# Linear attention's first head pair: TensorE's order written out, projections between its steps, two tiles' counts and the masks' last step on ScalarE

## The chip, the core and the metric

The kernel runs on one core of a Trainium2 chip. TensorE (PE) multiplies, VectorE (DVE), ScalarE (ACT) and GpSimd (POOL) do the rest, and SyncE (SP) issues transfers. Each engine works through its own instructions in the order in which they were built, and an instruction waits on semaphores until what it reads is there. The metric is the device time of one execution in microseconds (us); lower is better.

## The reference

One decoder layer over 1024 tokens of width 1024. What matters here is the first half: one projection feeds a sparse attention (group A), whose keys are chosen by an indexer's score, and a gated linear attention (group B).

```python
h = rmsnorm(x, norm1_g[l])
qa, ka, va, iq, ik, iw, qb, kb, vb, g_lr, r_gate = jnp.split(h @ w_in[l], split_points, axis=-1)
# group A: score = sum over 8 heads of relu(iq . ik) * iw, causal; the 256 best keys of each query are kept
_, idx = lax.top_k(score, topk)
...
# group B, in chunks: decayed attention inside a chunk, and a running state
log_a = jax.nn.log_sigmoid(g_lr @ gla_gate_w2[l] + gla_gate_b[l]) / GATE_TEMP
o_inter = einsum(qc * exp(b), state);  o_intra = einsum(attn, vc)       # b = cumsum(log_a)
state = exp(b_last) * state + einsum(kc * exp(b_last - b), vc)
o_b = rmsnorm(o_b, gla_out_norm_g[l]) * silu(r_gate)
x = x + concat([o_a, o_b]) @ w_out[l]
x = x + hier_moe(rmsnorm(x, norm2_g[l]), ...)                            # 32 experts
```

## The kernel before, in words

The 1024 tokens are 8 tiles of 128 (`t` = 0 to 7). The stage in question lies between the indexer's scores and the sparse attention, and three kinds of work meet in it.

**Projections.** `project_steps` makes one tile's projection onto 384 columns in 24 matmuls of 128x384 (weights split in a high part `wh` and a low part `wl`, 8 slices of each) into a PSUM tile `pj`, of which there are two. `load_w` brings a weight set in by DMA, makes `wh` on ACT (L259) and `wl` on DVE or POOL (L260). Of group B there are four sets: `qkv` and `vr`, for head pair 0 and head pair 1. `evac_qkv` copies a qkv projection out on ACT (`gq`, L402); `evac_vr` takes ACT for the value half and the output gate and ends on DVE (`gv`, L412).

**The linear attention** of a head pair `p` runs in four units `u` of two tiles. `gla1(p, u)` prepares: transposes of q and k (L616, L617), of the gate's low-rank input (L627), one gate matmul (L632), then a chain on ACT (`zb`, `l`: L636 to L639), DVE (`zb`, `l`, two cumulative sums `b` and `bc`: L641 to L647), POOL (ten subtractions `dd`: L653 to L658), ACT (exponentials: L660, L661) and DVE again (products with q and k: L669 to L675). `gla2(p, u)` uses them: five levels of small matmuls (L692 four times, L696), whose results DVE merges into `at` (L700, L705) and which take turns in three PSUM tiles `mm`; then the values and the state (L722, L725, L729; DVE updates the state at L733), the norm, and a `finish` that transposes the output (L752) and is called one unit later.

**The search.** For tiles 2 to 7 a threshold on the scores is searched in 7 rounds, `search(0)` to `search(6)`. A round counts, for each of the six tiles, the keys at or above a trial value (L512, one DVE instruction over 128 x (t+1)*128 with a sum, plus a read of that sum), and some 12 instructions on 128x6 choose the next value (L514 to L541). Rounds 0 to 4 count on a bf16 copy of the scores, 5 and 6 on the scores. `search_end` and `make_mask` then build each tile's mask; its last step is L578, on DVE.

What sets the order: inside a block `tc.manual_schedule(engines={PE})` PE's instructions keep the order in which they are written. Elsewhere a scheduler orders every engine by its own estimates. Before, the scoring ahead of this stage is such a block, with the rest of pair 0's qkv projections and all of its vr projections at its end; pair 0 of the linear attention, with pair 1's qkv projections and half of its vr projections, is not; pair 1 is again, and there a helper `weave` gives each step of `gla2` a room in nanoseconds that is filled with projections. Anything that is not PE's is the scheduler's throughout.

## Time and profile before

| | us |
|---|---|
| runs shown | 1091.1, 1083.46, 1087.89 (median 1087.89) |
| the profiled execution | 1083.67 |
| its span, first to last instruction | 1081.8 |
| PE busy | 997.9 (92%) |
| DVE busy | 777.4 (72%) |
| ACT busy | 657.3 (61%) |
| POOL busy | 387.7 (36%) |

The runs differ by 7.6 us, 0.7%. The stage that changes runs from the last matmul of the scores at 103.3 us to the first level matmul of pair 1 at 266.75 us. Times of rows are counted from the span's start. TensorE's granted clock is 1.00 at 2.4 GHz and 0.50 at 1.2 GHz.

### The profile page before, as it was taken

The page shows a single profiled execution, that of the slowest core. Times are in us where ns is not written, and L with a number is a line of the kernel's source. Part 1 is how long each engine was busy: PE and PEld are TensorE (multiplying, and loading weights), DVE is VectorE, ACT ScalarE, POOL GpSimd, SP SyncE. Part 2 cuts the span into 40 slices and gives each one's busy share as a digit, 9 for nine tenths or more (in the row PEclk, how much of TensorE's full clock was granted, in tenths as well). Part 3 has the DMA queues.
Part 4 walks back from the last instruction along what each step waited for, and adds up shares of the span by engine and source line. Part 5 has one row for each costly group of instructions (what it writes and reads, how often), then busy time and mean ns, then how long its engine had stood idle before and what let it go on. Part 6 is the DMA issues. An engine that isn't in the chain of part 4 may idle for free.

```text
span 1081.8 us, 17953 instructions
## 1 busy us (share of the span) xinstructions
PE 997.9 (92%) x5839; PEld 808.1 (75%) x5839; DVE 777.4 (72%) x2058; ACT 657.3 (61%) x1636; POOL 387.7 (36%) x497
## 2 busy tenths in 40 slices
PE   7799999989999999999989999949999999999993
PEld 7689888868888888988877878836666666666552
DVE  6877999874675666777775666667877777787772
ACT  7788643344655566666755533327877777777661
POOL 4510433641522224245442201154435444344321
PEclk9999999979999899999999999968999999999996
DMA  8210201020201202012231369869999999999983
GB/s 249 81 60 1 59 20 50 11 69 21 55 25 40 65 8 67 10 40 69 76 82 58 105 241 380 305 229 292 330 308 324 328 330 309 336 325 330 342 241 45
DMA packets 83204, 170.87 MB, mean 158 GB/s; under 512 B 14856, under 2 KB 45760, under 8 KB 82976
## 3 DMA queue, kind: packets, MB, share of 16 engines
q1 hardware_dynamic: 75936, 148.01, 40.6%
q0 software_dynamic: 7168, 21.65, 9.3%
q8 instruction: 48, 0.79, 0.3%
q14 instruction: 52, 0.43, 0.1%
HBM read 148.23 MB, written 26.88 MB: 162 GB/s over the span
## 4 chain that ended last, share of the span: by engine, by line
PE 57%; DMA 16%; DVE 14%; ACT 5%; issue 5%; POOL 1%; SPq 0%; POOLq 0%; DVEq 0%; ACTq 0%
PE pj L272 18%; DMA out_dram<-y,idx 9%; PE pj L1119 8%; DMA w<-in_w_exp_up_dram 4%; PE po L945 3%; PE mm L1493 3%; PE pj L1444 2%; PE pj L1446 2%; PE pj L1445 2%; DVE jb L512 2%; PE tp L933 2%; DVE w L1367 2%; DMA w<-in_w_exp_down_dram 2%; PE mm L1140 1%; PE mm L692 1%
## 5 line engine op out<-in xcount | busy, mean ns | idle before, releaser
L272 PE MATMUL pj<-wh,w 128*128 128x384 f32 (+1 forms) x1152 | 324.4, 348 | 7.2 <-DVE gv L412 6.1
L272 PEld LDWEIGHTS pj<-wh,w 128*128 128x128 f32 x1152 | 212.6, 194 | 15.6 <-DVE gv L412 7.6
L1366 ACT ACTIVATE w<-w 128x512 fp32r<-128x512 f32 x320 | 191.6, 627 | 45.7 <-PE mm L1446 27.9
L1367 DVE TENSOR_TENSOR w<-w,w 128x512 fp32r<-128x512 f32 x283 | 186.7, 698 | 31.5 <-ACT w L1366 28.2
L272 PE MATMUL pj<-wl,w 128*128 128x384 f32 (+1 forms) x576 | 200.1, 347 | 1.1 <-POOL wl L260 1.1
L272 PEld LDWEIGHTS pj<-wl,w 128*128 128x128 f32 x576 | 112.2, 195 | 4.5 <-POOL wl L260 1.3
L1444 PE MATMUL pj<-w,xT 128*96 128x512 f32 x256 | 105.7, 413 | 0.7 <-ACT w L1366 0.7
L1445 PE MATMUL pj<-w,xT 128*96 128x512 f32 x256 | 102.2, 399 | 1.6 <-DVE w L1367 1.1
L1446 PE MATMUL pj<-w,xT 128*96 128x512 f32 x256 | 102.0, 399 | 0.0
L1119 PE MATMUL pj<-w,mhl 128*128 128x512 f32 x384 | 101.1, 403 | 0.0
L910 POOL TENSOR_TENSOR cb<-bt,maskb 128x256 f32<-128x256 f32 (+1 forms) x64 | 43.5, 681 | 121.2 <-DVE mx L921 102.6
L1518 POOL DMA_INDIRECT out_dram<-y,idx x30 | 52.5, 1749 | 94.8 <-ACT w L1366 41.5
L260 POOL TENSOR_TENSOR wl<-wr,wh 128x384 fp32r<-128x384 f32 x58 | 60.8, 1070 | 61.9 <-ACT wh L259 61.6
L1119 PEld LDWEIGHTS pj<-w,mhl 128*128 128x128 f32 x384 | 69.4, 189 | 12.8 <-DVE mhl L1111 0.4
L1493 PE MATMUL mm<-w,hT 128*96 128x512 f32 x128 | 66.9, 605 | 0.5 <-ACT hT L1483 0.5
L1367 POOL TENSOR_TENSOR w<-w,w 128x512 fp32r<-128x512 f32 x37 | 50.4, 1361 | 46.5 <-ACT w L1366 36.0
L924 ACT ACTIVATE z<-z,mx 128x128 f32<-128x128 f32 (+7 forms) x64 | 49.5, 774 | 21.9 <-DVE mx L921 21.6
L1444 PEld LDWEIGHTS pj<-w,xT 128*96 128x96 f32 x256 | 44.1, 172 | 15.2 <-ACT w L1366 1.5
L1446 PEld LDWEIGHTS pj<-w,xT 128*96 128x96 f32 x256 | 41.9, 164 | 18.1 <-DVE xT L1458 0.2
L1445 PEld LDWEIGHTS pj<-w,xT 128*96 128x96 f32 x256 | 41.9, 164 | 17.2 <-DVE w L1367 2.6
L1454 PEld LDWEIGHTS tp<-cf,xg 96*128 96x128 f32 x256 | 40.9, 209 | 15.0 <-issue 8.5
L1444 PE MATMUL mm<-w,hTt 128*96 128x512 f32 x64 | 51.4, 804 | 0.0
(375 smaller groups left out, 2157.6 us busy)
## 6 DMA issues: line engine op xcount, KB each, us to landing
w<-in_w_exp_gate_dram SPq DMA_DIRECT2D x64, 512.0 KB
w<-in_w_exp_up_dram SPq DMA_DIRECT2D x64, 512.0 KB
w<-in_w_exp_down_dram SPq DMA_DIRECT2D x64, 512.0 KB
wr<-in_w_in_dram SPq DMA_DIRECT2D x80, 128.0 KB
xt<-in_x_dram SPq DMA_DIRECT2D x16, 512.0 KB
mt<-mixd SPq DMA_DIRECT2D x8, 512.0 KB
out_dram<-xt SPq DMA_DIRECT2D x8, 512.0 KB
h2d<-h SPq DMA_DIRECT2D x7, 528.0 KB
```

Of the source, the lines that this page charges most:

```text
L260: (V if by[kk + k] == "V" else G).tensor_tensor(b, raw[:, k], f32(a), op=OP.subtract)
L272: T.matmul(ps[:, :width], x_, y_[k], start=(k == 0 and i == 0), stop=(k == KC - 1 and i == 2))
L910: G.tensor_tensor(cb[:, :near], bts[p][:, i, 256 - near:], mask(t, far, L), op=OP.add)
L924: A.activation(z[:, :L], z[:, :L], AF.Exp, bias=mn, scale=-1.0, accum_out=sums[:, i:i + 1])
L1119: T.matmul(ps, lhs[:, k % 4], w[k, c], start=(k == 0 and i == 0), stop=(k == KC - 1 and i == 2))
L1366: A.activation(a, u, AF.Copy)
L1367: (G if engine == "G" else V).tensor_tensor(b, u, f32(a), op=OP.subtract)
L1444: T.matmul(ps, x[0], y[0], start=first, stop=False)
L1445: T.matmul(ps, x[0], y[1], start=False, stop=False)
L1446: T.matmul(ps, x[1], y[0], start=False, stop=last)
L1493: T.matmul(pd[:n], hT0, parts[2 * hf], start=True, stop=False)
L1518: G.indirect_dma_start(out=out[0], out_offset=bass.IndirectOffsetOnAxis(ap=idx[:CAP, e:e + 1], axis=0), in_=y[:CAP], in_offset=None, compu ...
```

## The change

1. The vr projections of pair 0 no longer stand at the end of the scoring block: that block now ends when pair 0's vr weights are loaded (`yield 0, "v"`).
2. Pair 0 of the linear attention becomes a written order of PE (`first_pair`), with what is left of the earlier filler, pair 1's qkv projections and half of its vr projections between its steps (`first_fill`). Each step of `gla2` gets 4.6 times its nominal room; the steps of `gla1` get their nominal room. A projection is held back until the step that frees its buffers has been written (`ended`).
3. `evac_qkv` copies q and k (`gq`) and v (`gw`) out with two ACT instructions in place of one.
4. In rounds 0 to 4 of the search the counts of tiles 6 and 7 (896 and 1024 keys) move to ACT, as a sum of signs; one DVE instruction on 128x2 turns the sums into counts.
5. The last step of each mask moves to ACT (a Relu with a large bias in place of a comparison and a product).

The constant behind the large bias is left out of the diff here.

```diff
@@ -74,6 +74,8 @@
 SHARE = (None, (1, 1, 1, 1, 1, 1, 0.85, 1.3), (1, 1, 1, 1, 1, 1, 0.85, 1.3), (1, 1, 1, 1, 1, 1, 1, 1.3))
 ROOM = (2.2, 2.8, 3.15, 3.3)
 OROOM = (0, 0, 0, 6000, 6000, 6000, 6000, 6000, 0)
+ROOM0 = (4.6, 4.6, 4.6, 4.6)
+MORE = 3
 LOG_FLOOR = -21.0 * 16.0
 LEVELS = (64, 32, 16, 8)
 BUCKET_START = [0, 1, 2, 3, 4, 5, 6, 7, 8, 9, 10, 11, 12, 13, 14, 15, 16, 19, 21, 24, 27, 31, 35, 40, 46, 52, 59,
...
@@ -234,7 +239,7 @@
     wp = p_h.enter_context(tc.tile_pool(name="wp", bufs=WBUFS, side="right"))
     hT = []
     p2 = ExitStack()
-    gqp = p2.enter_context(tc.tile_pool(name="gqp", bufs=10, side="right"))
+    gqp = p2.enter_context(tc.tile_pool(name="gqp", bufs=1, side="right"))
 
     p1 = ExitStack()
     scp = p1.enter_context(tc.tile_pool(name="scp", bufs=1, side="left"))
@@ -387,7 +392,7 @@
                         base=0, channel_multiplier=1)
 
 
-    gq, gv, pools = {}, {}, {}
+    gq, gw, gv, pools = {}, {}, {}, {}
 
     def qkv_load(p):
         c = p * P
@@ -398,8 +403,11 @@
         return load_w([(VB + 2 * c + P, P), (RG + 2 * c, 2 * P)], by=BY_VR[p])
 
     def evac_qkv(p, t, pj):
-        gq[p, t] = gqp.tile([P, 384], F32, name="gq", tag="gq", bufs=9)
-        A.activation(gq[p, t], pj[:, :384], AF.Copy, scale=rstd[:, t:t + 1])
+
+        gq[p, t] = gqp.tile([P, 256], F32, name="gq", tag="gq", bufs=NT)
+        gw[p, t] = gqp.tile([P, P], F32, name="gw", tag="gw", bufs=NT + MORE)
+        A.activation(gq[p, t], pj[:, :256], AF.Copy, scale=rstd[:, t:t + 1])
+        A.activation(gw[p, t], pj[:, 256:384], AF.Copy, scale=rstd[:, t:t + 1])
 
     def evac_vr(p, t, pj):
         g = pools["gvp"].tile([P, 384], F32, name="gv", tag="gv", bufs=NT)
@@ -455,6 +463,7 @@
                 index_operands(NT - 1)
                 yield 1000, NT - 1
         w = vr_load(0)
+        yield 0, "v"
         for t in range(NT):
             for ns in project_steps(t, w, lambda ps: evac_vr(0, t, ps)):
                 yield ns, 0
@@ -478,7 +487,7 @@
             score_sums(t)
             if t == 3:
                 relative_bias()
-        for _ in fill:
+        while next(fill)[1] != "v":
             pass
 
     p1b.close()
@@ -503,14 +512,29 @@
     V.tensor_tensor(st["v"], st["sd"], cf[:, CF_ZQ:CF_ZQ + 6], op=OP.mult)
     V.tensor_tensor(st["v"], st["v"], st["mean"], op=OP.add)
 
+    keys2 = srp.tile([P, 2], F32, name="keys2", bufs=1)
+    for t in range(6, NT):
+        G.memset(keys2[:, t - 6:t - 5], (t + 1) * P / 2)
+
     def search(it):
 
 
+        far = range(6, NT) if it < NROUND else ()
+        for t in far:
+
+            j = t - 2
+            jk = srp.tile([P, S], BF, name="ja", tag="ja", bufs=1)
+            A.activation(jk[:, :(t + 1) * P], mask(t), AF.Sign, bias=st["v"][:, j:j + 1], scale=-1.0,
+                         accum_out=st["c"][:, j:j + 1])
         for t in range(2, NT):
             j = t - 2
+            if t in far:
+                continue
             jk = srp.tile([P, S], BF, name="jb", tag="jb")
             V.tensor_scalar(jk[:, :(t + 1) * P], mask(t) if it < NROUND else acc[t], st["v"][:, j:j + 1], None,
                             op0=OP.is_ge, op1=OP.add, accum_out=st["c"][:, j:j + 1])
+        if far:
+            V.scalar_tensor_tensor(st["c"][:, 4:6], st["c"][:, 4:6], -0.5, keys2, op0=OP.mult, op1=OP.add)
         V.tensor_scalar(gei, st["c"], TARGET, None, op0=OP.is_ge)
         V.tensor_scalar(lti, st["c"], TARGET, None, op0=OP.is_lt)
         if it == NROUND:
@@ -575,7 +599,8 @@
         V.copy_predicated(k8, kp, m8)
         b2 = srp.tile([P, S], F32, name="b2", tag="jk")
         V.match_replace(b2[:, :L], k8, b1[:, :L], MARK)
-        V.tensor_scalar(mask(t), b2[:, :L], MARK_T, -NEG, op0=OP.is_gt, op1=OP.mult)
+
+        A.activation(mask(t), b2[:, :L], AF.Relu, scale=4e-9, bias=big)
 
 
     st_s = [glp.tile([P, P], F32, name=f"st_s{p}") for p in range(2)]
@@ -603,7 +628,7 @@
             room += ns
             while room > 0:
                 ns = next(fill, None)
-                if ns is None:
+                if not ns:
                     room = 0
                     break
                 room -= ns
@@ -717,7 +742,7 @@
         po = [ps[:, :2 * P].rearrange("p (i t) -> p i t", i=2) for ps in (ps_po(), ps_mm())]
         s = st_s[p]
         for i, t in enumerate(ts):
-            vals = (gq[p, t][:, 2 * P:], gv[p, t][:, :P])
+            vals = (gw[p, t], gv[p, t][:, :P])
             for h in range(2):
                 T.matmul(po[h][:, i], a[:, h, i], vals[h], start=True, stop=(t == 0))
             for h in range(2):
@@ -757,31 +782,59 @@
 
         gla_out[p] = finish
 
-    run(gla1(0, 0))
-    search(0)
-    search(1)
-    w = qkv_load(1)
-    run(gla1(0, 1))
-    for u in range(4):
-        run(gla2(0, u))
-        project_qkv(1, 2 * u, w)
-        project_qkv(1, 2 * u + 1, w)
-        if u < 2:
-            search(2 * u + 2)
-            search(2 * u + 3)
-            run(gla1(0, u + 2))
-        elif u == 2:
-            search(6)
-            search_end()
-            run(gla1(1, 0))
-    gla_out.pop(0)()
-    run(gla1(1, 1))
-    make_mask(2)
-    make_mask(3)
-    make_mask(4)
-    w = vr_load(1)
-    for t in range(4):
-        project_vr(1, t, w)
+    ended = [0, 0]
+
+    def first_pair():
+        yield from gla1(0, 0)
+        search(0)
+        search(1)
+        yield from gla1(0, 1)
+        ended[1] = 2
+        for u in range(4):
+            for ns in gla2(0, u):
+                yield ns * ROOM0[u]
+            ended[0] = u + 1
+            if u < 2:
+                search(2 * u + 2)
+                search(2 * u + 3)
+                yield from gla1(0, u + 2)
+                ended[1] = u + 3
+            elif u == 2:
+                search(6)
+                search_end()
+                yield from gla1(1, 0)
+        yield 2000
+        gla_out.pop(0)()
+        yield from gla1(1, 1)
+
+    ws = {}
+
+    def first_fill():
+
+        for ns, _ in fill0:
+            yield ns
+        w = qkv_load(1)
+        for t in range(NT):
+            while t >= MORE and ended[0] <= (t - MORE) // 2 or ended[1] <= t // 2:
+                yield 0
+            for ns in project_steps(t, w, lambda ps: evac_qkv(1, t, ps)):
+                yield ns if t else 2 * ns
+        w = ws["vr"] = vr_load(1)
+        for t in range(4):
+            while ended[0] <= t // 2:
+                yield 0
+            for ns in project_steps(t, w, lambda ps: evac_vr(1, t, ps)):
+                yield ns if t else 2 * ns
+
+    fill0 = fill
+    with tc.manual_schedule(engines={mybir.EngineType.PE}):
+        fill = first_fill()
+        weave(first_pair(), fill)
+        make_mask(2)
+        make_mask(3)
+        make_mask(4)
+        run(fill)
+    w = ws["vr"]
     for t in range(5, NT):
         make_mask(t)
```

**PE, behind the second gate matmul (u = 1) of pair 0, before.** `tp<-glT` is the gate matmul, `pj` rows are projections, `w4` and `w8` hold a tile's activations.

```order
L632 MATMUL tp_2000<-glT_2001,w2_106 128x256
L272 MATMUL pj_1613<-wh_1510,w4_255 128x384
L272 MATMUL pj_1613<-wl_1511,w4_255 128x384
L272 MATMUL pj_1613<-wh_1510,w4_256 128x384
L272 MATMUL pj_1613<-wh_1514,w4_255 128x384
L272 MATMUL pj_1613<-wl_1515,w4_255 128x384
L272 MATMUL pj_1613<-wh_1514,w4_256 128x384
L272 MATMUL pj_1613<-wh_1521,w4_255 128x384
L272 MATMUL pj_1613<-wl_1522,w4_255 128x384
L272 MATMUL pj_1613<-wh_1521,w4_256 128x384
```

These are the first nine of 24 projections that stand between that gate matmul and the first level matmul (L692).

**PE at the same place, after.** L657 is the gate matmul, L717 the level matmul, L277 the projection, L642 and L652 the last transposes of u = 1.

```order
L642 MATMUL tp_1726<-cf_64,gq_1339 128x128
L652 MATMUL tp_1733<-cf_64,glr_107 16x128 x2
L277 MATMUL pj_1625<-wh_1530,w8_133 128x384
L277 MATMUL pj_1625<-wh_1537,w8_133 128x384
L277 MATMUL pj_1625<-wl_1538,w8_133 128x384
L277 MATMUL pj_1625<-wh_1537,w8_133 128x384
L277 MATMUL pj_1625<-wh_1541,w8_133 128x384
L657 MATMUL tp_1733<-glT_1734,w2_106 128x256
L717 MATMUL mm_1788<-dd_1646 128x64
L717 MATMUL mm_1789<-dd_1646 128x64
L717 MATMUL mm_1788<-dd_1646 128x64
L717 MATMUL mm_1789<-dd_1646 128x64
```

The level matmuls of unit 0 now stand directly behind the gate matmul; the first gate matmul (u = 0) stands ahead of the rows shown, with five projections between the two, where 48 stood before.

**DVE, at the first gate's `zb`, before.** L512 is a count of round 0, L641 `zb` of unit 0, L646 its cumulative sum.

```order
L512 TENSOR_SCALAR jb,st_c<-maskb,st_v 128x640
L512 TENSOR_SCALAR jb,st_c<-maskb,st_v 128x768
L512 TENSOR_SCALAR jb,st_c<-maskb,st_v 128x896
L260 TENSOR_TENSOR wl<-wr,wh 128x384
L512 TENSOR_SCALAR jb,st_c<-maskb,st_v 128x1024
L641 SCALAR_TENSOR_TENSOR zb<-zb,l 128x256
L514 TENSOR_SCALAR gei<-st_c 128x6
L515 TENSOR_SCALAR lti<-st_c 128x6
L526 TENSOR_SCALAR st_num<-st_c 128x6
L642 TENSOR_SCALAR l<-zb 128x256
L646 SCALAR_TENSOR_TENSOR b<-zb 128x128 x2
```

The first gate's `zb` comes right behind round 0's counts.

**DVE at the same place, after.** L554 and L555 are the last steps of round 0, L534 a count of round 1, L666 `zb` of unit 0, L671 and L672 its cumulative sums.

```order
L552 TENSOR_TENSOR st_num<-st_num,st_sd 128x6
L553 TENSOR_TENSOR st_v<-st_v,st_num 128x6
L554 TENSOR_TENSOR st_v<-st_v,st_lo 128x6
L555 TENSOR_TENSOR st_v<-st_v,st_hi 128x6
L534 TENSOR_SCALAR jb,st_c<-maskb,st_v 128x384
L534 TENSOR_SCALAR jb,st_c<-maskb,st_v 128x512
L534 TENSOR_SCALAR jb,st_c<-maskb,st_v 128x640
L534 TENSOR_SCALAR jb,st_c<-maskb,st_v 128x768
L666 SCALAR_TENSOR_TENSOR zb<-zb,l 128x256
L667 TENSOR_SCALAR l<-zb 128x256
L671 SCALAR_TENSOR_TENSOR b<-zb 128x128 x2
L672 SCALAR_TENSOR_TENSOR bc<-l 128x128 x2
```

It now comes behind all of round 0 and the counts of round 1, which are four in place of six.

**ACT, on the first gate's chain, before.** L636 to L639 are the gate's four steps.

```order
L636 ACTIVATE zb<-tp,gs 128x256
L259 ACTIVATE wh<-wr 128x384 x2
L637 ACTIVATE l<-zb 128x256
L259 ACTIVATE wh<-wr 128x384
L638 ACTIVATE l<-l 128x256
L639 ACTIVATE l<-l 128x256
L619 ACTIVATE qk<-tp 128x512
L628 ACTIVATE glT<-tp 16x256
L663 ACTIVATE eb<-b 128x256
```

**ACT at the same place, after.** L661 to L664 are those four steps, L527 the counts by sign: the first row is round 0's second count, the other two are round 1's.

```order
L527 ACTIVATE ja,st_c<-maskb,st_v 128x1024
L661 ACTIVATE zb<-tp,gs 128x256
L644 ACTIVATE qk<-tp 128x512
L264 ACTIVATE wh<-wr 128x384
L662 ACTIVATE l<-zb 128x256
L653 ACTIVATE glT<-tp 16x256
L663 ACTIVATE l<-l 128x256
L527 ACTIVATE ja,st_c<-maskb,st_v 128x896
L664 ACTIVATE l<-l 128x256
L527 ACTIVATE ja,st_c<-maskb,st_v 128x1024
L688 ACTIVATE eb<-b 128x256
```

Round 1's first count stands ahead of the gate's last step (L664).

## Rows read from the trace of the kernel before

**Rows 1.** The page: the span, and TensorE's granted clock in 40 slices.
```profile
span 1081.8 us, 17953 instructions
...
PEclk9999999979999899999999999968999999999996
```

**Rows 2.** Busy us (xinstructions) of PE, PEld, DVE, ACT, POOL by stretch; clock, DMA share, GB/s.
```profile
104.00:267.00 163.00, 152.16 (x879) 133.92 (x879) 132.35 (x410) 71.73 (x187) 65.49 (x92) 0.93 0.14 36
104.00:132.00 28.00, 25.82 (x138) 24.28 (x137) 24.33 (x82) 17.43 (x42) 11.49 (x23) 0.94 0.23 57
132.00:180.00 48.00, 44.71 (x265) 40.06 (x264) 47.26 (x172) 18.94 (x50) 14.23 (x22) 0.96 0.14 34
```

**Rows 3.** What PE waited for from 104 to 267 us: total, times, longest.
```profile
PE pj L272 <- DVE gv L412: 6.1, 4, 2.2
PE tp L627 <- DVE st_s L733: 3.2, 1, 3.2
```

**Rows 4.** Timeline of PE: start us, us, engine line operation.
```profile
103.55 0.51 PE L272 MATMUL pj<-wh,w 128*128 128x384 f32 x2
...
113.70 0.69 PE L632 MATMUL tp<-glT,w 16*128 16x256 f32 x2
...
123.56 0.69 PE L632 MATMUL tp<-glT,w 16*128 16x256 f32 x2
126.43 0.54 PE L272 MATMUL pj<-wh,w 128*128 128x384 f32 x1 [2.18 <-DVE gv L412]
...
132.60 0.66 PE L692 MATMUL mm<-dd 64*128 64x64 f32 x8 [0.17 <-DVE dd L670]
...
266.75 0.66 PE L692 MATMUL mm<-dd 64*128 64x64 f32 x8
```

**Rows 5.** Timeline of DVE around the first gate.
```profile
114.24 0.61 DVE L512 TENSOR_SCALAR_CACHE_REDUCE jb<-maskb,st_v 128x384 bf16<-128x384 bf16 x1
...
117.17 1.14 DVE L512 TENSOR_SCALAR_CACHE_REDUCE jb<-maskb,st_v 128x896 bf16<-128x896 bf16 x1
...
119.91 0.42 DVE L641 SCALAR_TENSOR_TENSOR zb<-zb,l 128x256 f32<-128x256 f32 x1
...
124.69 0.61 DVE L512 TENSOR_SCALAR_CACHE_REDUCE jb<-maskb,st_v 128x384 bf16<-128x384 bf16 x1
...
131.97 0.29 DVE L669 TENSOR_TENSOR dd<-qk,dd 128x128 f32<-128x128 f32 x1
```

**Rows 6.** Timeline of ACT there.
```profile
107.20 0.95 ACT L365 ACTIVATE maskb<-acc 128x896 bf16<-128x896 f32 x1 [1.14 <-DVE acc L384]
108.06 0.19 ACT L365 ACTIVATION_READ_ACCUMULATOR maskb<-acc 128x1 f32 x1
...
118.69 0.42 ACT L639 ACTIVATE l<-l 128x256 f32<-128x256 f32 x1
...
127.16 1.47 ACT L661 ACTIVATE dd<-dd 128x1536 f32<-128x1536 f32 x1
```

**Rows 7.** Timeline of POOL there: first and last of ten subtractions.
```profile
121.48 0.66 POOL L653 TENSOR_TENSOR dd<-b 128x128 f32<-128x128 f32 x1 [1.81 <-DVE b L646]
...
125.53 0.61 POOL L658 TENSOR_TENSOR dd<-bc 128x256 f32<-128x256 f32 x1
```

**Rows 8.** Two stretches of low clock, columns as in the stretches above.
```profile
126.00:130.00 4.00, 3.57 (x12) 3.57 (x13) 4.00 (x8) 3.79 (x8) 1.37 (x4) 0.58 0.00 0
...
229.00:246.00 17.00, 15.97 (x63) 12.58 (x64) 10.37 (x33) 4.96 (x13) 0.98 (x3) 0.50 0.19 53
```

**Rows 9.** DVE's counts of tiles 7 and 6, grouped by line, 104 to 267 us.
```profile
L512 DVE TENSOR_SCALAR_CACHE_REDUCE jb<-maskb,st_v 128x1024 bf16<-128x1024 bf16 x5 | 6.4, 1275 | 0.0
...
L512 DVE TENSOR_SCALAR_CACHE_REDUCE jb<-maskb,st_v 128x896 bf16<-128x896 bf16 x5 | 5.7, 1137 | 0.0
```

**Rows 10.** The masks' last step on DVE: count, min/median/max ns, first and last start.
```profile
L578 DVE TENSOR_SCALAR maskb<-b x6: 353/590/854, 185.6 to 233.1; 128x384 bf16<-128x384 f32 x1, 128x512 bf16<-128x512 f32 x1, 128x640 bf16<-128x640 f32 x1, 128x768 bf16<-128x768 f32 x1
```

**Rows 11.** Timeline of DVE later, while POOL is busy too.
```profile
228.30 1.08 DVE L670 TENSOR_TENSOR dd<-qk,dd 128x128 f32<-128x128 f32 x1
```

More of the change, by code (lines that the diff above doesn't have):

```diff
@@ L90 @@
 CF_EPS = CF_IDENT + P
-CF_N = CF_EPS + 2
+CF_BIG = CF_EPS + 2
+CF_N = CF_BIG + 1
 CH_TRI = 0
@@ L119, in constants @@
     cf[:, CF_EPS:CF_EPS + 2] = EPS, 64 * EPS
+    cf[:, CF_BIG] = -NEG
     ch = np.zeros((P, CH_N), np.float32)
@@ L188, in layer @@
     eps = {EPS: cf[:, CF_EPS:CF_EPS + 1], 64 * EPS: cf[:, CF_EPS + 1:CF_EPS + 2]}
+    big = cf[:, CF_BIG:CF_BIG + 1]
     ch = const.tile([P, CH_N], F16, name="ch")
```

## The prediction

> **What bounds the kernel now.** I read the page first, then the stage that changes by stretches, then what PE waits for in it, then the timelines of PE, DVE, ACT and POOL around the first gate, where the new order differs most. The page shows TensorE at its high clock almost throughout, with a dip in the ninth of 40 slices, 216 to 243 us, which lies in this stage [rows 1]. In the whole stage, 104 to 267 us, PE is busy 152.16 of 163.00 us at a mean clock of 0.93 [rows 2]. So PE sets the end, and what can be won is bounded: 10.8 us of idle time, and 0.07 x 163 = 11.4 us that the clock took; the two overlap by about 1 us where PE idles at the low clock. I take 21.5 us as all that this stage loses. Between 132 and 180 us DVE is busy 47.26 of 48 us [rows 2], and PE's named waits end on DVE: on `gv` four times, 6.1 us together, once on the state, 3.2 us [rows 3]. PE is short of work only where DVE is full. After 2.18 us of idling at 124 us the clock is at 0.58 over the four following microseconds, and it is at 0.50 from 229 to 246 us [rows 4, 8]: an idle spell costs twice.
>
> **The change part by part.**
>
> *The same work.* Between the last score and the first level matmul of pair 1 (103.55 to 266.75 us, [rows 4]) both orders hold 563 projections and the same small matmuls, except that after also has the sixth gate matmul there, 0.6 us (a gate's two passes took 113.70 to 114.32). So the end moves by what the losses change, and by how cleanly the small matmuls are grouped. The new order issues all matmuls of a level together; before, the scheduler tore them into groups. I put that at a gain of 3 us (0 to 4), an estimate: some twenty places where a level or a value step is cut in two, at 0.16 us each. That is what starting a group anew costs: the first two projections of [rows 4] last 0.51 us, where each of the 58 up to the next row takes 10.15 / 58 = 0.175.
>
> *What is removed.* Ten counts leave DVE, five of 1.275 and five of 1.137 us, 12.1 us [rows 9], and six last mask steps of 0.35 to 0.85 us, 3.5 us [rows 10]: 15.6 us, of which five small instructions give back 0.5 to 1 us. DVE's relief is worth only what PE waits for DVE, and all its waits of the stage are inside the 10.8 us.
>
> *What is added on ACT.* No row shows the sign function. The nearest is a copy of 896 elements with a sum: 0.95 us and a read of the sum, of which 0.1 us adds up beside it [rows 6]. By it a pair of counts costs 2.1 to 2.3 us, ten 11 us. ACT is busy 71.73 of 163 us [rows 2] and has room for that, but not at once: what stands behind a count on ACT waits until the trial value is there. The Trainium skill, "ScalarE: Activation LUTs", section "What ACT_TABLE_LOAD costs", gives 280 ns and 0.833 ns for each element to an activation whose bias is a pointer; by that an estimate for a pair is 2.16 us. It falls inside the range of the rows, and the sum stays. The second copy in `evac_qkv` (some 0.2 us of ACT a tile) has ACT's idle time to hide in; without that, 16 tiles would make 3 us.
>
> *The new gap.* This is the dear term. PE has 58 + 5 projections from 103.55 us on, 0.175 us each, so it comes to the first gate matmul at 114.5 us, and after transposes and five more projections it stands at the second at 116.5 us. That one waits for a copy on ACT which now stands behind round 0's sign counts and `zb`; counting ACT's rows on, 119.6 us. Behind it come the level matmuls, with no projection ahead of them, and PE's order is fixed: all that is queued there, 182 of pair 0's 192 vr projections among it, waits too. They need DVE's products `dd`. In the trace the way from `zb` to the first product took from 119.91 to 131.97 us, 12.06 us [rows 5], with another round's counts in it as after has. When is `zb` after? Round 0's four counts take 114.24 to 117.17 = 2.93 us [rows 5]. Then DVE stands at a weight subtraction whose input ACT makes only behind its second count, to about 119.4 us; the round's small steps take some 1.6 us; round 1's four counts 2.93 more. That is 124.0 us, 4.1 later than before. The products are there at 136.0 us, and PE idles from 116.5 to 136.0 less 0.6 of gate: 18.9 us. Lower end: no wait at the weight subtraction (`zb` at 121.5), and the way shortened to what it holds, 1.6 us to the cumulative sum, ten subtractions on POOL from 121.48 to 126.14 [rows 7], the exponentials (1.47 us, [rows 6]) and 1 us of queues: 9 us; then PE idles 14 us. Upper end: round 2's pair on ACT ahead of the exponentials, 2 us more: 21 us. I take 18.5, nearest the trace's own way.
>
> *The clock behind it.* In the trace 2.18 us of idling is followed by 2 x (1 - 0.58) x 4 = 3.4 us at half speed, which cost 1.7 us [rows 4, 8]. I take the same. The other end is the long spell, 17 us at 0.50: 8.5 us [rows 8].
>
> *Unit 0 while DVE still searches.* From 136 to 166 us I followed both queues: PE needs 0.6 us for a level and 14 projections, 2.5 us; DVE has rounds 3 to 6 and the merges between them. A projection tile needs `pj` free, hence DVE's `gv` behind three counts, and level 5 needs a merge behind two: 0.6 and 1.2 us of waiting, 1.8 in all (0 to 4).
>
> *Units 1 to 3.* DVE now has 12.1 us less of search ahead of the masks [rows 9] and mostly keeps pace. Twice PE passes from one weight set to the next, and POOL's subtractions for the new one stand around the mask's first step; I count 2 us. Where POOL works beside it, DVE's product of 0.29 us [rows 5] takes 1.08 [rows 11]; once in unit 1 that makes DVE late by 1 to 2 us. Together 3.5 us (1 to 8), with 0.5 us at pair 0's last transpose.
>
> *Sum.* Losses after: 18.5 + 1.7 + 1.8 + 4.0 = 26.0 us, against 21.5: +4.5; the sixth gate +0.6; cleaner groups -3.0: +2.1 us. From pair 1 on the order is as before. Against the profiled execution's 1083.67 us that is 1085.8. That execution lay 0.4% below the median of the runs shown, so I give 1089 (1087.89 + 2.1 is 1090; I lean 1 us to the better side, since the gap's lower end is the farther one).
>
> **The rivals.**
>
> *Faster.* The gap is at its lower end (14 us) and units 1 to 3 lose 1 us, since DVE is freed of 12.1 us of counting and the merges come in time: 26.0 - 4.5 - 3.0 - 1.8 = 16.7, so 4.8 - 2.4 = 7.2 us faster, 1081. For it: the low spell from 229 to 246 us came of DVE's backlog, and there is none then. Against: it needs `zb` at 121.5 us on a DVE that is full.
>
> *Slower.* The clock does not come back after the gap. The mechanism: in unit 0 each level hangs on DVE's counts, PE stands again and again for a microsecond, as it did for 3.2 us at once on the state [rows 3] ahead of the long spell, and TensorE runs at 1.2 GHz for 17 us or more [rows 8]: +6.8 us, with the gap at its upper end +2.5 and unit 0 at its end +2.2: 13.6 us slower in all, 1101. It decides from about 10 us of half clock on. For it: the longest idle time of the stage is new. Against: unlike in the long spell, 14 projections stand between two levels. The Trainium skill, "TensorE: Matmul & The Clock Gate", section "Why this matters for your kernels", advises against idle time between bursts of matmuls, since the engine then restarts at its lower clock; that speaks against this order, and the trace agrees [rows 4, 8]. It gives no time that the rows don't.
>
> *The change does not do what it says.* If DVE's relief and the gap lay beside other work, nothing would change: 1088. For the gap that can't be, since PE's queue stands.
>
> **How the numbers follow.** I give the forecast (within 6 us of 1089) 0.55, the faster rival 0.25, the slower one 0.20. 1%, 10.9 us, is about what a measurement of this kernel can tell from no change. The faster rival lies 3 to 4 us short of it; with something under half of it and a little of the forecast beyond, faster by over 1% gets 0.13. Most of the slower rival and the upper edge of the forecast lie beyond 1% on the other side: 0.20. Within 1%: 0.67. The range goes from the faster rival with another 3 us, 1078, to the slower one less a little, 1099.
>
> **What would show it.** In the changed profile: PE idle for 14 to 21 us between about 116 and 136 us, ended by DVE `dd`, with half clock for 3 us behind it; DVE's `zb` of unit 0 near 124 us; DVE's last search round over near 165 us; no half clock near 229 to 246 us; the first level matmul of pair 1 at 264 to 271 us. It is wrong if the gap is much shorter than 14 us, if half clock lasts beyond 10 us behind it, or if a wait of more than 3 us stands in units 1 to 3.

## The result: slower by 3%

The changed kernel takes 1120.21 us in the median (1117.21 to 1121.72, 4 runs), the kernel before 1087.68 beside it (1083.46 to 1091.10): 1.0302 times as long, interval 1.0277 to 1.0328, +32.5 us. The prediction said 1089, at most 1099. Two more measurements of the same kernel gave 1.0300 and 1.0346.

The page of the changed kernel (line, then what [rows 1] shows of before) has PE busy for about as long as before, 1002.4 us against 997.9; what grew is the time in which it stood or ran at the low clock.

```profile
span 1118.1 us, 17984 instructions
PE 1002.4 (90%) x5839; PEld 811.5 (73%) x5839; DVE 766.7 (69%) x2037; ACT 675.8 (60%) x1678; POOL 391.6 (35%) x499
PEclk9999689999799899999998999968999999989987
```

What PE waited for from 104 to 285 us, in the same columns as [rows 3]. The first row is the new gap, the third holds a wait of 4.6 us that nothing in the prediction speaks of.

```profile
PE mm L717 <- DVE dd L695: 18.3, 1, 18.3
PE mm L721 <- DVE at L725: 6.0, 4, 3.2
PE pj L277 <- DVE gv L420: 5.7, 3, 4.6
PE tp L652 <- ACT zb L661: 3.2, 1, 3.2
```

The timeline of PE, which answers to [rows 4]: the first gate comes at 114.82 us (113.70 before), the first level matmul at 140.32 (132.60 before), the first of pair 1 at 284.91 (266.75 before), one projection behind a wait of 4.57 us.

```profile
114.82 0.69 PE L657 MATMUL tp<-glT,w 16*128 16x256 f32 x2
...
119.28 0.39 PE L652 MATMUL tp<-cf,glr 128*16 128x128 f32 x2 [3.17 <-ACT zb L661]
...
120.83 1.22 PE L657 MATMUL tp<-glT,w 16*128 16x256 f32 x2
140.32 1.12 PE L717 MATMUL mm<-dd 64*128 64x64 f32 x8 [18.27 <-DVE dd L695]
...
284.29 0.69 PE L277 MATMUL pj<-wh,w 128*128 128x384 f32 x1 [4.57 <-DVE gv L420]
284.91 1.12 PE L717 MATMUL mm<-dd 64*128 64x64 f32 x8
```

Stretches of the changed kernel, columns as in [rows 2]. Both places at which PE stands are followed by half clock (0.50): from 120 to 143.5 us, most of it while PE idles, and from 285 to 297 us, while PE is busy all the time, which is 6 us lost.

```profile
120.00:143.50 23.50, 5.23 (x21) 3.98 (x20) 23.12 (x73) 12.59 (x24) 13.59 (x27) 0.50 0.07 17
160.00:165.00 5.00, 4.88 (x22) 4.76 (x23) 4.96 (x20) 0.00 (x0) 0.00 (x0) 0.66 0.01 3
285.00:297.00 12.00, 12.00 (x51) 10.62 (x51) 1.88 (x7) 0.54 (x2) 0.00 (x0) 0.50 0.00 0
```

**The gap, engine by engine.** DVE's `zb` and its products (the rows that answer to [rows 5]), then ACT between them. `zb` is at 124.40 us, the first product at 139.04: 14.64 us, where [rows 5] had 12.06. POOL had the last subtraction ready at about 130.3 us. ACT had stood since 128.0 us at a sign count whose trial value DVE had not made yet; it got on at 130.77, did the two counts, and came to the exponentials at 133.08 and 133.99. They ended at 135.5, and DVE came to the products 3.6 us later, behind its round's small steps.

```profile
124.40 0.42 DVE L666 SCALAR_TENSOR_TENSOR zb<-zb,l 128x256 f32<-128x256 f32 x1
...
139.04 0.40 DVE L694 TENSOR_TENSOR dd<-qk,dd 128x128 f32<-128x128 f32 x1
```
```profile
130.77 1.04 ACT L527 ACTIVATE ja<-maskb,st_v 128x896 bf16<-128x896 bf16 x1 [2.78 <-DVE st_v L562]
131.71 0.19 ACT L527 ACTIVATION_READ_ACCUMULATOR ja<-maskb,st_v 128x1 f32 x1
131.93 1.15 ACT L527 ACTIVATE ja<-maskb,st_v 128x1024 bf16<-128x1024 bf16 x1
...
133.08 0.40 ACT L685 ACTIVATE en<-dd 128x256 f32<-128x256 f32 x1
...
133.99 1.47 ACT L686 ACTIVATE dd<-dd 128x1536 f32<-128x1536 f32 x1
```

**The branch.** Behind the first pair DVE reads a flag and branches on it; the body behind the branch is not run. These are DVE's rows there, of the kernel before and then of the changed one. In both DVE does nothing for 4 to 6 us around the branch. Before, pair 1's second gate stood behind all this on PE, at 268.94 us, so that only a `gv` was left for DVE behind the branch. In the changed kernel that gate, the sixth, is at 265.04 us, ahead of the flag. Its exponentials are done at 277.19 us, while DVE is at the branch, and its ten products, 2.3 us, come behind the branch and ahead of the `gv` for which PE stands.

```profile
261.27 0.15 DVE L794 CAST flag<-pj 1x1 int32<-1x1 f32 x1 [2.23 <-PE pj L792]
265.37 0.48 DVE L412 SCALAR_TENSOR_TENSOR gv<-pj,rstd,gv 128x256 f32<-128x256 f32 x1 [3.95 <-DVEq L796]
```
```profile
275.08 0.14 DVE L847 CAST flag<-pj 1x1 int32<-1x1 f32 x1 [2.10 <-PE pj L845]
275.22 0.43 DVE L700 TENSOR_TENSOR en<-qk,en 128x256 f32<-128x256 f32 x1
281.47 0.29 DVE L694 TENSOR_TENSOR dd<-qk,dd 128x128 f32<-128x128 f32 x1 [5.82 <-ACT gv L419]
...
283.76 0.47 DVE L420 SCALAR_TENSOR_TENSOR gv<-pj,rstd,gv 128x256 f32<-128x256 f32 x1
```

The products are only a part of that wait. DVE stands 3.95 us in before and 5.82 in the changed kernel; in e2 (below), which has the changed order and the ten products behind the branch too, it stands 3.59, and PE's wait there is 2.36 us, not 4.57.

```profile
282.37 0.29 DVE L694 TENSOR_TENSOR dd<-qk,dd 128x128 f32<-128x128 f32 x1 [3.59 <-DVEq L849]
```

The changed kernel's row names ACT's `gv` as what ended the 5.82 us. In e8, the same kernel, the step that is named had ended 0.37 us before DVE went on, and the next one had not ended. What does differ is how often instructions are fetched between the branch and DVE's next instruction: once in before (262.0 to 265.4 us) and in e2 (279.0 to 282.3), twice in the changed kernel (276.0 to 281.4). The rows of the instruction queue, in that order:

```profile
q14 instruction: 1, 0.01, 0.9%
```
```profile
q14 instruction: 1, 0.01, 0.9%
```
```profile
q14 instruction: 2, 0.02, 1.1%
```

It is once in e1, e4, e5, e10, e11 and e12 as well, which stand 3.8 to 4.3 us, and twice in e3, e8, e9, e13 and e14, which stand 5.6 to 6.4. So some 2.2 us of the 4.57 go with the second fetch. No run moves that fetch alone.

**How far the loss goes.** The attention's last score, the same instruction in both kernels, is at 625.40 and at 650.68 us: 25.3 us of the difference are there (19.6 and 22.5 in e8 and e13, two more executions of the changed kernel). The rest of it comes behind the attention.

```profile
625.40 0.22 PE L916 MATMUL mm<-kT,qp 128*128 128x128 f32 x1
```
```profile
650.68 0.22 PE L969 MATMUL mm<-kT,qp 128*128 128x128 f32 x1
```

### The profile page after: what moved, and what is told of

Same layout as the page of the kernel before. It is cut to its first block, busy times and chain, and to the rows that moved or that the text cites. A ratio compares the mean times of both kernels' runs of the same rounds, so it can differ in the third digit from the quotient of the medians.

```text
span 1118.1 us, 17984 instructions
## 1 busy us (share of the span) xinstructions
PE 1002.4 (90%) x5839; PEld 811.5 (73%) x5839; DVE 766.7 (69%) x2037; ACT 675.8 (60%) x1678; POOL 391.6 (35%) x499
## 5 line engine op out<-in xcount | busy, mean ns | idle before, releaser
L277 PE MATMUL pj<-wh,w 128*128 128x384 f32 (+1 forms) x1152 | 326.7, 351 | 7.0 <-DVE gv L420 5.7
L277 PEld LDWEIGHTS pj<-wh,w 128*128 128x128 f32 x1152 | 213.4, 195 | 16.5 <-DVE gv L420 6.6
L1420 DVE TENSOR_TENSOR w<-w,w 128x512 fp32r<-128x512 f32 x283 | 187.5, 700 | 37.6 <-ACT w L1419 36.5
L277 PE MATMUL pj<-wl,w 128*128 128x384 f32 (+1 forms) x576 | 201.0, 349 | 1.1 <-POOL wl L265 1.1
L277 PEld LDWEIGHTS pj<-wl,w 128*128 128x128 f32 x576 | 113.1, 196 | 4.1 <-POOL wl L265 1.3
L1498 PE MATMUL pj<-w,xT 128*96 128x512 f32 x256 | 103.5, 404 | 5.7 <-POOL w L1420 4.6
L1497 PE MATMUL pj<-w,xT 128*96 128x512 f32 x256 | 107.1, 419 | 0.5 <-ACT w L1419 0.4
L1499 PE MATMUL pj<-w,xT 128*96 128x512 f32 x256 | 103.2, 403 | 0.0
L1571 POOL DMA_INDIRECT out_dram<-y,idx x30 | 58.3, 1945 | 99.0 <-ACT w L1419 35.2
L1420 POOL TENSOR_TENSOR w<-w,w 128x512 fp32r<-128x512 f32 x37 | 50.7, 1369 | 45.1 <-ACT w L1419 44.1
L1499 PEld LDWEIGHTS pj<-w,xT 128*96 128x96 f32 x256 | 42.6, 166 | 18.5 <-DVE xT L1511 0.2
## 6 DMA issues: line engine op xcount, KB each, us to landing
wr<-in_w_in_dram SPq DMA_DIRECT2D x80, 128.0 KB, 2.6
```

The lines of the kernel that those rows point to most:

```text
L277: T.matmul(ps[:, :width], x_, y_[k], start=(k == 0 and i == 0), stop=(k == KC - 1 and i == 2))
L1420: (G if engine == "G" else V).tensor_tensor(b, u, f32(a), op=OP.subtract)
L1497: T.matmul(ps, x[0], y[0], start=first, stop=False)
L1498: T.matmul(ps, x[0], y[1], start=False, stop=False)
L1499: T.matmul(ps, x[1], y[0], start=False, stop=last)
L1571: G.indirect_dma_start(out=out[0], out_offset=bass.IndirectOffsetOnAxis(ap=idx[:CAP, e:e + 1], axis=0), in_=y[:CAP], in_offset=None, compu ...
```

## The experiments

Theory A: the loss is the written order's, at two places, the gap ahead of the first level matmul and the branch. Theory B: ACT's new counts are to blame. Theory C: DVE sets the pace, so that waits only move. This table of marks read from each profiled execution (us from its start) serves all of them. "Ratio" is to the kernel before, with its interval.

| kernel | first level matmul | pair 1's first | attention's last score | from there to the end | ratio |
|---|---|---|---|---|---|
| before | 132.60 | 266.75 | 625.40 | 456.4 | 1 |
| changed | 140.32 | 284.91 | 650.68 | 467.4 | 1.0302 (1.0277 to 1.0328) |
| e1 | 138.47 | 260.21 | 618.61 | 464.9 | 0.9952 (0.9925 to 0.9978) |
| e2 | 134.12 | 285.73 | 653.26 | 461.6 | 1.0226 (1.0192 to 1.0259) |
| e3 | 153.88 | 276.86 | 638.80 | 468.7 | 1.0152 (1.0118 to 1.0186) |
| e4 | 141.53 | 284.56 | 639.46 | 470.7 | 1.0214 (1.0166 to 1.0263) |
| e5 | 152.20 | 273.18 | 627.38 | 467.3 | 1.0072 (1.0035 to 1.0108) |
| e6 | 135.22 | 281.57 | 639.89 | 465.5 | 1.0198 (1.0112 to 1.0285) |
| e7 | 140.35 | 278.64 | 632.81 | 473.7 | 1.0188 (1.0119 to 1.0256) |
| e8 | 141.87 | 282.82 | 645.00 | 468.6 | 1.0300 (1.0238 to 1.0362) |
| e9 | 141.95 | 285.60 | 650.75 | 468.3 | 1.0213 (1.0178 to 1.0248) |
| e10 | 154.33 | 275.53 | 628.99 | 465.8 | 1.0068 (1.0040 to 1.0095) |
| e11 | 137.66 | 264.94 | 625.32 | 459.5 | 0.9971 (0.9943 to 0.9999) |
| e12 | 135.72 | 259.51 | 619.41 | 462.5 | 1.0054 (1.0021 to 1.0087) |
| e13 | 141.68 | 284.54 | 647.89 | 460.8 | 1.0346 (1.0294 to 1.0398) |
| e14 | 140.46 | 285.44 | 649.52 | 457.9 | 1.0292 (1.0238 to 1.0346) |

In e4, e5, e7 and e10 a tile of 24 projections more stands ahead of pair 1's first level matmul; for these the attention's mark is the one to compare. Each mark is of one execution: at the attention's last score the changed kernel and its repeats e8 and e13 differ by up to 5.7 us, and e1 and e11, whose order on PE is the same, by 6.7. Smaller differences there decide nothing.

**e1, the arithmetic without the order.** The kernel before with the diff's lines of `search` and `make_mask` (and their constants), nothing else.

> The kernel before with only the arithmetic moved: ten sign counts and the masks' last step on ACT, order and buffers as before. Theory A (the loss of 32 us is the written order's: PE's queue stands in front of the level matmuls, and pair 1's products fall behind the branch): within 6 us of before, 1082 to 1094, and no wait of PE over 4 us in the stage. Theory B (ACT's new counts are to blame, since copies and exponentials queue behind them): slower than before by 10 us or more, 1098 and up.

0.9952: theory B falls as the cause of the loss. ACT's counts and the masks' step alone gain some 4 to 5 us (1084.51 against 1088.45).

**e2, the order without the arithmetic.**

```diff
-        far = range(6, NT) if it < NROUND else ()
+        far = ()
...
-        A.activation(mask(t), b2[:, :L], AF.Relu, scale=4e-9, bias=big)
+        V.tensor_scalar(mask(t), b2[:, :L], MARK_T, -NEG, op0=OP.is_gt, op1=OP.mult)
```

> The changed kernel with all counts and the masks' last step back on DVE, the written order kept. Theory A: the gap ahead of the first level matmul stays at 16 to 22 us and the time within 8 us of the changed kernel, 1112 to 1128. Theory B: most of the loss goes, 1088 to 1100.

1114.48 us: the order alone, with the split copies and the buffers that go with it, loses most of it, as theory A says. But the gap was expected at 16 to 22 us and its two waits are 2.45 and 11.81 us. PE there:

```profile
118.96 0.60 PE L652 MATMUL tp<-cf,glr 128*16 128x128 f32 x2 [2.45 <-ACT zb L661]
...
134.12 1.12 PE L717 MATMUL mm<-dd 64*128 64x64 f32 x8 [11.81 <-DVE dd L695]
```

So the sign counts that stand on ACT ahead of the exponentials make the gap 6.2 us longer (140.32 less 134.12). With all counts on DVE the same time is lost later, in waits for merges: at pair 1's first level and at the attention's last score e2 is no earlier than the changed kernel. In these two executions its 6 us lie behind the attention (461.6 us there instead of 467.4); but the changed kernel itself took 460.8 to 468.6 us there (e13, e8), so where they are won is not shown.

**e3, a filled gap.** Projections of pair 0's vr set in front of the gates' successors, and fewer between the later levels.

```diff
-ROOM0 = (4.6, 4.6, 4.6, 4.6)
+ROOM0 = (3.2, 3.2, 3.2, 3.2)
...
         yield from gla1(0, 0)
+        yield 3000
         search(0)
         search(1)
         yield from gla1(0, 1)
         ended[1] = 2
+        yield 18000
```

> The changed kernel with 18 more projections ahead of the second gate and 108 more ahead of the first level matmul, and fewer between the later levels. If PE's queue is what costs there (theory A): the gap of 18.3 us falls under 4 us, no half clock at 120 to 143 us, and the first level matmul of pair 1 comes 12 to 18 us earlier than at 284.9; in all 1102 to 1110. If DVE sets the stage's pace (theory C): the gap closes, but as much waiting comes back between the levels of units 0 and 1, and pair 1 starts within 5 us of 284.9; 1114 to 1122.

1106.58 us, within theory A's range; pair 1's mark is 8 us earlier, not 12 to 18. The wait ahead of the level matmul is gone, but PE now stands where these projections are evacuated, since `gv` on DVE is queued behind the counts (two of the three waits of the first row, 2.67 and 5.35 us, are within the former gap; the third is the branch):

```profile
PE pj L277 <- DVE gv L420: 12.7, 3, 5.4
PE po L750 <- DVE st_s L758: 3.6, 1, 3.6
```

Both theories hold in part: 13.6 us of the time are won, though 8.0 us of waiting for DVE have come back.

**e4, the flag later.** The branch's flag comes one tile of projections after where it was.

```diff
-        for t in range(4):
+        for t in range(5):
             while ended[0] <= t // 2:
...
-        for t in range(4, NT):
+        for t in range(5, NT):
             yield from project_steps(t, w, lambda ps: evac_vr(1, t, ps))
```

> The changed kernel with one more tile of projections (24) between pair 1's second gate and the flag, so that its products stand ahead of the branch on DVE. If the wait of 4.6 us at 284 us and the 13.6 us of half clock around it come of that place (theory A): both go, and the time falls by 7 to 12 us, to 1108 to 1113. If the half clock there has another cause (theory D): only the wait goes, 1114 to 1118, or nothing does.

1111.92 us, 8.3 below the changed kernel, as theory A says. The sixth gate's products now stand ahead of the flag on DVE, and behind the branch there is only `gv`, as in before (and a single instruction fetch):

```profile
276.71 0.29 DVE L694 TENSOR_TENSOR dd<-qk,dd 128x128 f32<-128x128 f32 x1 [1.64 <-ACT dd L686]
...
279.73 0.15 DVE L847 CAST flag<-pj 1x1 int32<-1x1 f32 x1 [0.26 <-PE pj L845]
283.65 0.48 DVE L420 SCALAR_TENSOR_TENSOR gv<-pj,rstd,gv 128x256 f32<-128x256 f32 x1 [3.77 <-DVEq L849]
```

PE waits nowhere longer than 1.0 us there, its clock stays at 1.00 from 198 to 364 us, and the attention's last score comes 11.2 us earlier (5.5 and 8.4 against e8 and e13). The half clock at 285 to 297 us thus came of the wait at the branch.

**e5, both.** The diffs of e3 and e4 together.

> The filled gap and the later flag together in the changed kernel. If the two losses are of separate places (theory A), the gains add: 13.6 and 8.3 us off 1120, so 1098 (1094 to 1103), and no wait over 2 us next to the branch. If the stage's waits are one sum that only moves (theory C): 1104 to 1110.

1094.88 us: the gains add. At the attention's last score the kernel is 2.0 us behind before, not 25.3: the two places in the order carry nearly all of what the trace shows there. Against e1 and e11, which have its arithmetic without the written order, it is 8.8 and 2.1 us behind.

**e6, early gates, and e7, all three.** In e6 the first two gates go ahead of the 63 projections that close the scores' stage (42 of them now stand between the second gate and the level matmul).

```diff
-        while next(fill)[1] != "v":
-            pass
...
         yield from gla1(0, 0)
-        search(0)
-        search(1)
         yield from gla1(0, 1)
         ended[1] = 2
+        yield 10500
+        search(0)
+        search(1)
```

> The changed kernel with the first two gate matmuls ahead of the last projections of the scores' stage instead of behind them; nothing else is moved. Theory A (the gap is as long as the way from the gate to the products, and the gate is at the wrong place): products 5 to 10 us earlier, the wait ahead of the first level matmul 8 to 14 us instead of 18.3, 1108 to 1115. Theory E (DVE's counts decide when the products come, wherever the gate stands): the first level matmul within 3 us of 140, 1117 to 1122.

1105.32 us, a little better than theory A's range. The gate doesn't come ten microseconds earlier: it waits 4.6 us for ACT's copy, and DVE's `zb` is at 116.78 instead of 124.40. The wait ahead of the level matmul is 9.5 us; it ends at 135.22.

e7 adds e4's edit and fills the rest of the gap with 91 projections (`yield 15000`, `ROOM0` 4.3).

> Early gates, 91 projections between the second gate and the first level matmul, and the later flag. Theory A: the waits of the front and of the branch are nearly gone, pair 1's first level matmul at 258 to 268 us (with a tile more in front of it), 1084 to 1096. Theory C: DVE's counts bring as much waiting back between the levels, 1098 to 1106.

Missed: 1107.98 us. No wait for the products is left, yet PE waits 4.9 us for split weights from POOL and 4.0 us for `gv`, and the first gate 4.6 us for ACT. At the attention's last score it is 7.4 us behind before, where e5 is 2.0 behind; the time lies outside both ranges, nearer to theory C's.

**e8, the changed kernel again,** with nothing altered.

> The changed kernel once more, with nothing altered. 1117 to 1122 us. Its attention ends some 25 us later than before's, but its end is 36 us later. If those 11 us more are a chance of the two profiled executions: from the end of the attention to the end of the span 456 to 463 us this time. If they belong to the change: 466 to 470 us again.

1118.06 us, and 468.6 us behind the attention, as if that belonged to the change. Why should it? The code behind is the same, but its order on ACT, DVE and POOL is the scheduler's, by its own reckoning of time, and that was shifted. Among POOL's instructions of that stage two pairs have changed places. One is the scatter of an expert's output (L1518 before, L1571 after) and a subtraction that makes a weight's low part (L1367, L1420). POOL's order before, then after:

```
412 L1462 TENSOR_TENSOR gate<-xg,minef 96x1
413 L1367 TENSOR_TENSOR w_12566<-w_11939,w_12566 128x512
414 L1518 DMA out_dram<-y,idx 1024x1024
```
```
413 L1515 TENSOR_TENSOR gate<-xg,minef 96x1
414 L1571 DMA out_dram<-y,idx 1024x1024
415 L1420 TENSOR_TENSOR w_12609<-w_11982,w_12609 128x512
```

The timeline of POOL in e8 there, and PE's row that waits:

```profile
1037.23 4.72 POOL L1571 DMA_INDIRECT out_dram<-y,idx  x1 [3.42 <-ACT w L1419]
1041.52 1.73 POOL L1420 TENSOR_TENSOR w<-w,w 128x512 fp32r<-128x512 f32 x1
```
```profile
1043.30 0.47 PE L1498 MATMUL pj<-w,xT 128*96 128x512 f32 x1 [3.45 <-POOL w L1420]
```

e3 to e7 have this swap; before, e1 and e2 don't.

**e9, that scatter put back,** in the changed kernel; **e10** is the same in e5.

```diff
+            with tc.issue_after(on_pool[33].ins) if e == 25 else ExitStack():
+                G.indirect_dma_start(out=out[0], ...
```

> The changed kernel, with one scatter on POOL near the end put back behind the weight subtraction that stood ahead of it in before. Theory F (the written order of the first pair also moved what is scheduled 700 us later, and a scatter of 4.7 us in front of that subtraction makes PE wait 3.5 us, with half clock behind): one of the two waits of 3.5 us in the last 60 us goes, the stretch from the end of the attention to the end of the span takes 459 to 465 us instead of 467.4 and 468.6, and the time is 3 to 7 us below the changed kernel's. Rival (chance of the executions): 466 to 470 us, same time.

> Filled gap, later flag and the scatter put back, all three in the changed kernel. Theory A and F: 3 to 7 us below the 1094.9 of the first two alone, so 1088 to 1092, the time of the kernel before (0.998 to 1.005). Rival: 1094 to 1098.

The edit did more than put one scatter back: in e9, e10 and e14 the next scatter stands behind its subtraction too (1063.75 and 1061.42 us in e9), while before has that scatter first (1026.08 and 1027.36). e9 was 1.0213 times before, 8 us under e8, more than expected; but in its profiled execution, the slowest of its kernel, the stretch took 468.3 us, and the wait was shortened to 1.95 us, not gone: the subtraction itself took 4.23 us there. e10 was 1.0068 against e5's 1.0072: nothing gained.

**e11, the arithmetic alone (e1) with the next scatter behind its subtraction** (index 34, `e == 26`), and **e12, e1 without the masks' step.**

> The kernel before with the arithmetic on ACT alone (0.9952), and the scatter after next to the end put behind its weight subtraction: there a scatter of 4.7 us stood ahead of a wait of 3.46 us on PE. Theory F: that wait goes, 1080 to 1082, ratio 0.992. Rival (the subtraction waits for its weights anyway): 0.994 to 0.997 as without it.

> The kernel before with the sign counts on ACT, the masks' last step left on DVE. If the counts carry the gain of the two (12.1 us of DVE against 3.5): 0.994 to 0.998. If the masks' step does: 0.999 to 1.003.

e11: the wait of 3.46 us is gone, the time isn't lower (0.9971). e12: 1.0054, outside both expectations. Up to the attention's last score it is as fast as e1 (619.41 and 618.61 us). Behind it POOL's order differs: e12 has both swaps of the changed kernel, without its written order, while e2 has the written order without the swaps. In e12 the scatter at 1023.37 us takes 4.13 us and PE waits 3.55 us behind it; but e1, without a swap, has such a place too (4.72 and 3.46 us), and e12's profiled execution, one of its fastest, took 462.5 us behind the attention, e1's 464.9. So that the swaps make e12 slower than e1 is not shown; both lie within 1% of before.

**e13 and e14** time the changed kernel and e9 side by side.

> The changed kernel, nothing altered, in five rounds beside the next one. 1117 to 1121 us, ratio 1.029 to 1.032.

> The changed kernel with the one scatter put back behind the weight subtraction, in five rounds beside the run before this. Theory F: 5 to 10 us below it, ratio 1.020 to 1.025, and 459 to 465 us from the end of the attention to the end. Rival (the stage behind is set by the stream of weights and the clock, and the waits only move): within 3 us of it, and 466 to 470 us.

1.0346 and 1.0292, with intervals that overlap. e14 is lower by some 6 us in the median (1122.38 and 1116.73), as in e9; but behind the attention the changed kernel took 460.8 us this time and e14 457.9. That stretch thus varies from execution to execution (460.8 to 468.6 us for the same kernel), and the scatter's place is worth somewhere between nothing (e10) and some 8 us (e9 under e8). It stays open.

## Why the prediction was wrong

**The step that failed** is the sixth gate: "except that after also has the sixth gate matmul there, 0.6 us", and "From pair 1 on the order is as before". I priced the moved gate by its matmul on PE alone. What follows from it on the other engines moved with it: ten products on DVE, from behind the first level of pair 1 to the place where DVE is held by the branch. That costs 4.57 + 0.24 us of waiting, and then the clock is at half until 297.5 us, 6.6 us more: 11.4 us where the sum has 0.6. e4 shows it: 11.2 us less at the attention's last score, 8.3 in the time. No rival spoke of that place. Its size is in part chance: some 2.2 us of the wait go with the second instruction fetch, and in e8, the same kernel, 4.42 us of waiting are followed by 6.8 us of half clock, which makes 8.1 us in place of 11.4.

**The other terms of the sum**, each with what it measured:
- *The gap*: 18.5 us (14 to 21) was forecast, 3.17 + 18.27 = 21.4 was measured. `zb` came at 124.40 us, 124.0 was forecast. The way from `zb` to the products was the mis-sized part: "round 2's pair on ACT ahead of the exponentials, 2 us more" was named as the upper end. ACT also waits for the pair's trial value, and the products then stand behind the small steps of DVE's round; by e2 the counts on ACT lengthen the gap by 6.2 us.
- *The clock behind it*: 1.7 us. Half clock lasts from 140.3 to 143.9 us, so 1.8: right. It was low already between PE's two waits, from 120.0 us, where the gate matmul took 1.22 us in place of 0.69; that is some 1.0 us that the sum doesn't have. The pair of sign counts, from 130.77 to 133.08 us, is as reckoned (2.1 to 2.3). The Trainium skill, "ScalarE: Activation LUTs", section "What ACT_TABLE_LOAD costs", gives an activation whose bias is a pointer 280 ns and 0.833 ns for each element, an estimate of 1.03 and 1.13 us for 896 and 1024. The trace agrees to 2% (1.04 and 1.15 us); the two reads of the sums come on top, beside other work.
- *Unit 0*: 1.8 us (0 to 4). Waits of 0.43, 0.93 and 0.64 us, 2.0 in all; but from 160.9 us the clock is at half for 3.4 us, 1.7 more, which I had not counted for so short waits: 3.7.
- *Units 1 to 3*: 4.0 us (1 to 8). Waits of 6.9 us (3.15 the longest, for a merge in unit 1) and half clock for 3.4 us: 8.6, past the upper end.
- *Sixth gate and cleaner groups*: +0.6 and -3.0 us. They aren't measured by themselves, and the 0.16 us behind the -3.0 is no price of a group: in the middle of a stream a pair of projections lasts 0.51 us as well, while the next one starts 0.34 us after it (113.69 and 114.03 us in the changed kernel), so the rest overlaps. Losses after of 21.4 + 1.0 + 1.8 + 3.7 + 8.6 + 11.4 = 47.9 us against the 21.5 of before, less 2.4, make +24.0; the attention's first score is at 355.00 and 377.79 us, +22.8. The terms account for that stage to about 1 us, with the 2.4 unmeasured.
- *Two slips* changed little: the faster rival's "4.8 - 2.4" has to be a sum, its 7.2 is right, and the gap's lower end leaves out the 0.6 us of the gate (13.4 us, not 14).

**From the stage to the time.** The prediction took the difference at the stage's end over into the time unchanged. It is 22.8 us where the attention begins, 25.3 at its last score, and 32.5 in the medians. Behind the attention each kernel's stretch differs from execution to execution by up to 10 us; a possible cause is the swap on POOL (theory F), whose price the runs leave between nothing and some 8 us. What makes these last 7 us stays open. The profiled execution of before, the shortest behind its attention, took 456.4 us there, so the profiles alone overstate that part.

**What was right**: that DVE's relief is worth little (e1: 4 to 5 us), that the gap is the dear term and is ended by `dd`, that no half clock is left at 229 to 246 us, and that an idle spell costs twice. The "slower" rival had the sign and the wrong place: the clock stays low not behind the gap, but behind the wait at the branch, where 13.7 us of half clock come with 4.6 us of waiting. The prediction's own test "a wait of more than 3 us stands in units 1 to 3" turned out against it (3.15 us).

**A better version.** e1 is the fastest that was run, 0.9952 of before: the arithmetic without the order. With the written order mended (e5) the kernel is still 0.7% slower than before. I read it so that the scheduler's order lets PE go round DVE's queue, which a written one can't; no run shows that by itself.

## What to carry to other kernels

When an engine's order is written out, follow the others' queues to the end of the stage and one step beyond. A branch held DVE for 3.6 to 6.4 us here, and a step that is moved to such a place has to be priced on every engine that its results pass through. Filling a gap with work helps less where that work's results leave through the engine that made the gap (in e3 8.0 us of waiting came back). And where another engine's order is a scheduler's, a change at one place can swap instructions far behind, with or without a written order (the changed kernel and e12); compare the orders of the whole program, not of the stage.

## What the runs showed of the hardware that was not expected

- DVE stands idle around a branch whose body isn't run: for 3.95, 3.59 and 3.77 us in before, e2 and e4, with one fetch of instructions between the branch and DVE's next instruction, and for 5.82, 5.66 and 6.13 us in the changed kernel, e8 and e13, with two.
- The issue of a scatter on POOL takes 1.4 to 2.3 us as a rule (all of before's) and 4.1 to 4.7 us in some places, at 1037.23 us of e8 for one; in e9 the subtraction put in front of it took 4.23 us instead of 1.7. What slows POOL there was not found.
- After waits of under 1 us in unit 0 PE's clock went to 0.50 for 3.4 us (0.66 over the five microseconds from 160 us), and with one of 4.57 us for 13.7 us, though PE was busy from the wait's end on. The length doesn't go with the wait's: it was 13.7 us with 2.36 us of waiting in e2 and 6.8 us with 4.42 us in e8.
